# Twelve low parts of weight sums in each of three FFNs, written by ScalarE and an accumulating DMA in place of VectorE

## The chip, the cores and the metric

The kernel runs on one core of a Trainium2 chip. The metric is the device time of one execution in microseconds (us). PE is the matrix engine (TensorE), DVE is VectorE, ACT is ScalarE, POOL is GpSimd, and SP is the engine whose queue issues most of the loads.

## What is computed

The reference is a two-layer decoder trunk for 576 tokens (one sequence of 512, and eight of 8) of width 1024. Each layer is a token mixer between two half-step SwiGLU FFNs, so there are four FFNs, named (layer, place): (0,0), (0,1), (1,0), (1,1). The change is in the FFNs alone:

```python
def swiglu(h, w_gate, w_up, w_down):
    return (jax.nn.silu(h @ w_gate) * (h @ w_up)) @ w_down
...
x = x + 0.5 * swiglu(rmsnorm(x, ffn_norm[i, 0]), ffn_w_gate[i, 0], ffn_w_up[i, 0], ffn_w_down[i, 0])
```

`w_gate` and `w_up` are 1024 x 2816, `w_down` is 2816 x 1024, all float32.

## The kernel before

**Split numbers.** A float32 product is made from three matmuls of reduced operands: each operand is split into a high part (a cast to fp32r) and a low part (source minus high), and high x high, high x low and low x high are summed in PSUM. `block` (L321) does that for one 128 x 512 weight block: it takes a tile `wb` from a pool, ACT casts the high part into its first half (L326), and an engine, DVE if none is named, writes the low part `src - hi` into its second half (L327). `wb` comes from the pool `spl` with six buffers.

**Strassen products.** The gate and up projections of an FFN run over 11 column pairs, p = 0 to 10 (L541), each of 256 columns of both matrices. A pair is worked by `wino` (L373) in seven products instead of eight. `prod(i, slot)` is one product: for gate and for up, one `wb` block and 12 matmuls of 128 x 288 (L384), 24 matmuls in all. The products come in the order 0, 1, 3, 2, 4, 5, 6. Products 0, 1 and 2 read the loaded weights `raw`; products 3, 4, 5 and 6 read sums of them, `ws`, which POOL makes in `prep` (L362 to L365, four for each matrix: s0, s1, s2 and s3; product 4 reads s0, 5 reads s2, 6 reads s3). After each product DVE or ACT empties the PSUM bank (L389, L394); there are three PSUM tiles for this. `gate` (L550, L551, and the split in L418 and L419) makes the activations of the pair.

**Buffers and queues.** `load` (L330) fetches 1 MB of `w_gate` or `w_up` for a pair on SP's queue (L334) into `raw`, which has two buffers; `ws` has six. So the load for the next pair goes out when the last reader of the older one is done, and a weight sum is made when the sum whose buffer it takes has been read. After the pairs p = 2, 4, 6 and 8, `down` (L348 are its matmuls, L425 its sum into `x`) multiplies four finished columns of the activations by `w_down`; its low parts are written on POOL.

**Which FFNs.** In (0,0), (0,1) and (1,1), called plain in the code, pair 0 takes a direct path without sums (L556 to L578, the PSUM tiles emptied at L575), and the pairs 1 to 10 go through `wino`. In (1,0) all eleven do.

**What sets the order.** The program is written in the order of the loops, and the tile framework's scheduler reorders each engine's instructions within what the data and the buffers allow, by a simulated timeline (`schedule_with_timeline_sim=True`). A few instructions are pinned by `pin`. The ring for descriptors of DMAs that POOL issues is set by `dynamic_dma_scratch_size=1024`; the kernel before issues no DMA from POOL.

Of the kernel before, what the change touches and what calls it, by code (L numbers as in the profile page):

```python
# [8 lines left out]
F32 = mybir.dt.float32  # L9
F32R = mybir.dt.float32r  # L10
I32 = mybir.dt.int32
AF = mybir.ActivationFunctionType
ALU = mybir.AluOpType
# [5 lines left out]
D = 1024  # L19
# [30 lines left out]
def trunk(ctx, tc, x_prompt, x_sample, state_ssm, state_conv, state_pool,  # L50
# [5 lines left out]
    V, S, G, PE = nc.vector, nc.scalar, nc.gpsimd, nc.tensor  # L56
# [196 lines left out]
    def pin(op, on=True):  # L253
        if on:
            tc.keep_in_program_order(op)
# [64 lines left out]
    def block(src, eng=None, pool=None, late=False):  # L320
        w = (pool or spl).tile([P, 2, 4, P], F32R, name="wb")  # L321
        k = src.shape[1]
        hi, lo = w[:, 0, 0:k], w[:, 1, 0:k]
        if src.ndim == 4:
            hi, lo = [a.rearrange("p k (c f) -> p k c f", c=src.shape[2]) for a in (hi, lo)]
        S.copy(out=hi, in_=src)  # L326
        pin((eng or V).tensor_tensor(out=lo, in0=src, in1=hi.bitcast(F32), op=ALU.subtract), late)  # L327
        return w

    def load(src, shape):  # L330
# [39 lines left out]
                w[i, m] = block(src[i])  # L370
        return st, w

    def wino(wp, pre, out, hh, done, early):  # L373
        st, w = pre
        e1, e4, u2, t5 = [wp.tile([P, 2, HALF], F32, name=n) for n in ("e1", "e4", "u2", "t5")]

        def prod(i, slot):
            pt = acc_tile()
            for m in range(2):
                wb = w[i, m] if (i, m) in w else block(st[m][i])  # L380
                n = 0
                for k in range(4):
                    for j, h in ((0, 0), (0, 1), (1, 0)):
                        PE.matmul(out=pt[:, m, 0:HALF], lhsT=wb[:, j, k], rhs=hh[k, h][:, slot], start=n == 0, stop=n == 11)  # L384
                        n += 1
            return pt[:, :, 0:HALF]

        def add(o, a, b, e=V):
            e.tensor_tensor(out=o, in0=a, in1=b, op=ALU.add)  # L389

        def scale(e, o, h):
            e.tensor_tensor(out=o, in0=o, in1=psum["rb"][h].unsqueeze(1).broadcast_to(list(o.shape)), op=ALU.mult)  # L392

        S.copy(out=e1, in_=prod(0, 0))  # L394
        c11 = out[:, :, 0, 0]
        add(c11, prod(1, 1), e1)
        add(u2, prod(3, 4), e1)
        add(e4, prod(2, 6), u2)
        if early:
            early()  # L400
        scale(V, c11, 0)
        add(t5, prod(4, 3), u2)
        p7 = prod(5, 5)
        add(out[:, :, 1, 0], p7, e4)
        add(out[:, :, 1, 1], p7, t5)
        c12 = out[:, :, 0, 1]
        for h in range(2):
            scale(V, out[:, :, 1, h], h)
        done(1)
        add(c12, prod(6, 2), t5)  # L410
        scale(V, c12, 1)
        done(0)
# [84 lines left out]
    def ffn(i, s, pools, tail):  # L497
        gp, dp, fp = pools
        wg, wu, wd = kview(ffn_w_gate[i, s]), kview(ffn_w_up[i, s]), kview(ffn_w_down[i, s])

        def start(p, n):
            return prep(fp, [load(w[:, :, p * 256:(p + 1) * 256], (8, 256)) for w in (wg, wu)], n)

        plain = (i, s) != (1, 0)
# [20 lines left out]
        else:  # L525
            pre = start(0, 4)
        with ExitStack() as hs:
            hp = hs.enter_context(tc.tile_pool(name="h", bufs=1, side="right", reuse_waits="tile"))
            sqs = None
            if i + s:  # L530
                sqs = tail()
# [3 lines left out]
            hh = next(norms)  # L535
# [7 lines left out]
            for p in range(11):  # L543
                ghi = gp.tile([P, 2, T], F32R, name="ghi")
                glo = gp.tile([P, 2, T], F32R, name="glo")
                o = fp.tile([P, 2, 2, 2, HALF], F32, name="fo")
# [8 lines left out]
                if p == 0 and plain:  # L555
                    for j, h in ((0, 0), (0, 1), (1, 1), (1, 0)):  # L556
# [4 lines left out]
                        for q in range(2):  # L561
                            slot = (0, 1, 5, 2)[2 * h + q]
                            for m in range(2):
                                wb = wq[q][m]
# [4 lines left out]
                        src = pt[:, :, 0:HALF]  # L569
                        if j == 0 and i + s:  # L570
                            src = o[:, :, j, h]
# [5 lines left out]
                            gate(j)  # L577
                    next(norms)  # L578
                else:
                    wino(fp, pre if p == 0 else start(p, 0), o, hh, gate, None if p else lambda: rnorm(sqs and rnat2(sqs, D), True))  # L580
                if p % 2 == 0 and 0 < p < 10:
                    k0 = 2 * p - 4
                    down(dp, wd, k0, 4, [g[k0 + k] for k in range(4)], (0, 1, 2, 3), 0.5, False, lo_eng=G, late=p == 2)
# [652 lines left out]
```

## Time and profile before

| | us |
|---|---|
| median of the three runs | 2339.83 |
| lowest and highest run | 2336.1, 2342.46 |
| the profiled execution | 2337.29 |
| its span in the trace | 2335.6 |
| PE busy in the span | 2274.0 (97%) |
| DVE busy | 1828.9 (78%) |
| ACT busy | 1062.1 (45%) |
| POOL busy | 1030.9 (44%) |

The span is the stretch from the first to the last instruction of the profiled execution, which took 1.7 us more than its span. The engines run at the same time, so busy times don't add up to the span. A timeline row groups neighbouring instructions of one kind: its start, its length, engine, line and tile names (without buffer numbers), the count, and in square brackets how long the engine was idle before it and what ended that. A row that counts fewer matmuls than the program has can miss a record.

In the trace the second pair of FFN (0,0) begins at about 49 us, the third at about 72 us; the same stretches of (0,1) and (1,1) lie near 1040 to 1085 us and 1960 to 2005 us.

### The profile page before, as it was taken

How to read it: one execution, taken by the hardware profiler on the slowest of the kernel's cores; microseconds unless marked ns; L12 is line 12 of the kernel's file. 1: busy time of each engine (PE TensorE's matmuls, PEld its weight loads, DVE VectorE, ACT ScalarE, POOL GpSimd, SP SyncE). 2: the span in 40 equal slices, each digit the busy share in tenths (PEclk: the TensorE clock that was granted, in tenths of full speed). 3: DMA queues.
4: the chain of work that ended last, by engine and by line, in shares of the span. 5: the costliest groups of instructions: out<-in, count | busy, mean ns of one | idle time of the engine just before them, and what ended most of it. 6: DMA issues, size and time to landing. Idle time of an engine off the chain costs nothing.

```text
span 2335.6 us, 43763 instructions
## 1 busy us (share of the span) xinstructions
PE 2274.0 (97%) x17572; PEld 2233.1 (96%) x17572; DVE 1828.9 (78%) x2870; ACT 1062.1 (45%) x2004; POOL 1030.9 (44%) x796
## 2 busy tenths in 40 slices
PE   8999999999999999999999999999999999999998
PEld 7999999989999999889999999999999899999997
DVE  7887778578887777797887799777876769778866
ACT  6444335465555544443444365333443345344433
POOL 3655440334444444255555335645531325645530
PEclk9999999999999999999999999999999999999998
DMA  4323232243444443322223232332221232322221
GB/s 133 109 91 109 73 100 66 62 136 115 141 121 117 122 128 102 110 73 90 92 91 109 64 100 82 100 108 64 91 91 59 73 96 91 109 90 77 88 73 59
DMA packets 272903, 222.23 MB, mean 95 GB/s; under 512 B 8321, under 2 KB 269041, under 8 KB 272700
## 3 DMA queue, kind: packets, MB, share of 16 engines
q1 hardware_dynamic: 269172, 218.04, 30.6%
q8 instruction: 139, 2.28, 0.4%
q10 hardware_dynamic: 3528, 1.39, 0.2%
q14 instruction: 64, 0.52, 0.1%
HBM read 206.46 MB, written 12.94 MB: 94 GB/s over the span
## 4 chain that ended last, share of the span: by engine, by line
PE 74%; DVE 16%; ACT 3%; DMA 3%; issue 2%; POOL 2%; ACTq 0%; SPq 0%; DVEq 0%; POOLq 0%
PE acc L348 37%; PE acc L384 31%; DVE wb L327 4%; DVE cacc L660 1%; DVE wh L263 1%; DMA raw<-in_ffn_w_gate 1%; DVE wh L274 1%; PE acc L488 1%; POOL wb L327 1%; DVE fo L392 1%; DVE fo L389 1%; ACT m L831 1%; DVE fo L551 1%; PE misc L888 1%; DMA raw<-in_ffn_w_up 1%
## 5 line engine op out<-in xcount | busy, mean ns | idle before, releaser
L384 PE MATMUL acc<-wh,wb 128*128 128x288 f32 x6888 | 922.8, 295 | 15.1 <-DVE fo L389 5.8
L384 PEld LDWEIGHTS acc<-wh,wb 128*128 128x128 f32 x6888 | 916.0, 188 | 19.3 <-DVE wb L327 7.3
L348 PE MATMUL acc<-ghi,wb 128*128 128x288 f32 x2752 | 552.3, 295 | 6.3 <-DVE x L425 3.5
L348 PEld LDWEIGHTS acc<-ghi,wb 128*128 128x128 f32 x2752 | 441.6, 188 | 8.2 <-DVE x L425 4.4
L326 ACT CAST wb<-raw 128x512 fp32r<-128x512 f32 (+1 forms) x440 | 265.4, 607 | 352.4 <-PE acc L348 142.9
L348 PE MATMUL acc<-glo,wb 128*128 128x288 f32 x1376 | 404.2, 295 | 0.0
L348 PE MATMUL acc<-hhi,wb 128*128 128x288 f32 x1824 | 382.8, 299 | 3.3 <-DVE x L425 0.9
L327 POOL TENSOR_TENSOR wb<-raw,wb 128x512 fp32r<-128x512 f32 (+1 forms) x154 | 211.0, 1372 | 342.6 <-ACT wb L326 330.6
L327 DVE TENSOR_TENSOR wb<-ws,wb 128x512 fp32r<-128x512 f32 x328 | 328.3, 1012 | 18.1 <-ACT wb L326 17.7
L327 DVE TENSOR_TENSOR wb<-raw,wb 128x512 fp32r<-128x512 f32 (+1 forms) x286 | 274.3, 973 | 68.3 <-ACT wb L326 67.7
L326 ACT CAST wb<-ws 128x512 fp32r<-128x512 f32 x328 | 201.4, 620 | 258.4 <-PE acc L384 202.2
L348 PEld LDWEIGHTS acc<-hhi,wb 128*128 128x128 f32 x1824 | 296.8, 189 | 5.7 <-DVE x L425 1.1
L348 PE MATMUL acc<-hlo,wb 128*128 128x288 f32 x912 | 271.6, 298 | 0.0
L425 DVE SCALAR_TENSOR_TENSOR x<-acc,x 128x576 f32<-128x576 f32 x160 | 120.7, 754 | 192.0 <-PE acc L348 191.7
L365 POOL TENSOR_TENSOR ws<-raw,ws 128x512 f32<-128x512 f32 x82 | 154.8, 1888 | 243.7 <-DVE wb L327 239.4
L348 PEld LDWEIGHTS acc<-glo,wb 128*128 128x128 f32 x1376 | 257.8, 188 | 0.0
L327 POOL TENSOR_TENSOR wb<-rd,wb 128x512 fp32r<-128x512 f32 x128 | 177.4, 1398 | 161.5 <-ACT wb L326 161.5
L326 ACT CAST wb<-rd 128x512 fp32r<-128x512 f32 x196 | 113.9, 592 | 246.5 <-PE acc L348 217.5
L364 POOL TENSOR_TENSOR ws<-raw 128x512 f32<-128x512 f32 x82 | 125.2, 1526 | 166.0 <-DVE wb L327 166.0
L348 PEld LDWEIGHTS acc<-hlo,wb 128*128 128x128 f32 x912 | 172.1, 189 | 0.7 <-issue 0.2
L362 POOL TENSOR_TENSOR ws<-raw 128x512 f32<-128x512 f32 x82 | 127.2, 1552 | 70.2 <-DMA raw<-in_ffn_w_gate 66.3
L363 POOL TENSOR_TENSOR ws<-ws,raw 128x512 f32<-128x512 f32 x82 | 130.7, 1594 | 6.1
(337 smaller groups left out, 2837.9 us busy)
## 6 DMA issues: line engine op xcount, KB each, us to landing
raw<-in_ffn_w_gate SPq DMA_DIRECT2D x41, 1024.0 KB
raw<-in_ffn_w_up SPq DMA_DIRECT2D x41, 1024.0 KB
rd<-in_ffn_w_down SPq DMA_DIRECT2D x80, 512.0 KB
raw<-in_ssd_w_in SPq DMA_DIRECT2D x48, 512.0 KB
m<-ad SPq DMA_DIRECT2D x16, 576.0 KB
nat<-in_state_ssm SPq DMA_DIRECT2D x16, 512.0 KB
out<-nat SPq DMA_DIRECT2D x16, 512.0 KB
raw<-in_ssd_w_out SPq DMA_DIRECT2D x24, 256.0 KB
```

The costliest lines, as they stand in the source:

```text
L263: return V.scalar_tensor_tensor(out=o, in0=xs, scalar=g, in1=sub, op0=ALU.mult, op1=ALU.subtract)
L274: (G if slot == 3 else V).tensor_tensor(out=hh[k, 1][:, slot], in0=t[k][slot], in1=hi.bitcast(F32), op=ALU.subtract)
L326: S.copy(out=hi, in_=src)
L327: pin((eng or V).tensor_tensor(out=lo, in0=src, in1=hi.bitcast(F32), op=ALU.subtract), late)
L348: PE.matmul(out=pd[:, h, 0:HALF], lhsT=lt, rhs=a[:, h * HALF:(h + 1) * HALF], start=first and n == 0, stop=last and n == 3 * len(acts) - 1)
L362: G.tensor_tensor(out=s[0], in0=blk[2], in1=blk[3], op=ALU.add)
L363: G.tensor_tensor(out=s[1], in0=s[0], in1=blk[0], op=ALU.subtract)
L364: G.tensor_tensor(out=s[2], in0=blk[2], in1=blk[0], op=ALU.subtract)
L365: G.tensor_tensor(out=s[3], in0=blk[1], in1=s[1], op=ALU.subtract)
L384: PE.matmul(out=pt[:, m, 0:HALF], lhsT=wb[:, j, k], rhs=hh[k, h][:, slot], start=n == 0, stop=n == 11)
L389: e.tensor_tensor(out=o, in0=a, in1=b, op=ALU.add)
L425: V.scalar_tensor_tensor(out=halves(x[:, d]), in0=pt[:, :, 0:HALF], scalar=scale, in1=halves(x[:, d]), op0=ALU.mult, op1=ALU.add)
```

## The change

For products 4, 5 and 6 of the pairs p = 1 and 2 in the three plain FFNs the low part is written in another way. ACT writes the negated high part into the low half of `wb` (L328 of the changed kernel), and POOL issues a DMA that adds the source `ws` onto it (L329): 128 rows of 2 KB, 256 KB. The value is the same, `src - hi`. Two matrices by three products by two pairs by three FFNs are 36 blocks: 36 DVE instructions go, 36 ACT instructions and 36 DMAs come. From L327 on the changed kernel's lines stand four further down (L365 is L369, L384 is L388).

```diff
--- before.py
+++ after.py
@@ -324,7 +324,11 @@
         if src.ndim == 4:
             hi, lo = [a.rearrange("p k (c f) -> p k c f", c=src.shape[2]) for a in (hi, lo)]
         S.copy(out=hi, in_=src)
-        pin((eng or V).tensor_tensor(out=lo, in0=src, in1=hi.bitcast(F32), op=ALU.subtract), late)
+        if eng == "dma":
+            S.activation(out=lo, in_=hi.bitcast(F32), func=AF.Identity, scale=-1.0)
+            G.dma_start(out=lo.bitcast(F32), in_=src, accum_op=ALU.add)
+        else:
+            pin((eng or V).tensor_tensor(out=lo, in0=src, in1=hi.bitcast(F32), op=ALU.subtract), late)
         return w
 
     def load(src, shape):
@@ -370,14 +374,14 @@
                 w[i, m] = block(src[i])
         return st, w
 
-    def wino(wp, pre, out, hh, done, early):
+    def wino(wp, pre, out, hh, done, early, up=None):
         st, w = pre
         e1, e4, u2, t5 = [wp.tile([P, 2, HALF], F32, name=n) for n in ("e1", "e4", "u2", "t5")]
 
         def prod(i, slot):
             pt = acc_tile()
             for m in range(2):
-                wb = w[i, m] if (i, m) in w else block(st[m][i])
+                wb = w[i, m] if (i, m) in w else block(st[m][i], up if i > 3 else None)
                 n = 0
                 for k in range(4):
                     for j, h in ((0, 0), (0, 1), (1, 0)):
@@ -577,7 +581,7 @@
                             gate(j)
                     next(norms)
                 else:
-                    wino(fp, pre if p == 0 else start(p, 0), o, hh, gate, None if p else lambda: rnorm(sqs and rnat2(sqs, D), True))
+                    wino(fp, pre if p == 0 else start(p, 0), o, hh, gate, None if p else lambda: rnorm(sqs and rnat2(sqs, D), True), "dma" if plain and p < 3 else None)
                 if p % 2 == 0 and 0 < p < 10:
                     k0 = 2 * p - 4
                     down(dp, wd, k0, 4, [g[k0 + k] for k in range(4)], (0, 1, 2, 3), 0.5, False, lo_eng=G, late=p == 2)
```

The scheduler moves instructions near these blocks. Three places, in FFN (0,0). The number behind a tile's name tells its buffers apart; numbers of the two kernels don't match.

**POOL, second pair.** Before, the last two sums of the pair (ws_575, ws_576), then those of the third pair, from raw_825 (gate) and raw_827 (up), then the low parts of `down`:

```order
L364 TENSOR_TENSOR ws_575<-raw_563 128x512
L365 TENSOR_TENSOR ws_576<-raw_563,ws_574 128x512
L362 TENSOR_TENSOR ws_829<-raw_825 128x512
L363 TENSOR_TENSOR ws_830<-ws_829,raw_825 128x512
L364 TENSOR_TENSOR ws_831<-raw_825 128x512
L365 TENSOR_TENSOR ws_832<-raw_825,ws_830 128x512
L362 TENSOR_TENSOR ws_837<-raw_827 128x512
L363 TENSOR_TENSOR ws_838<-ws_837,raw_827 128x512
L364 TENSOR_TENSOR ws_839<-raw_827 128x512
L365 TENSOR_TENSOR ws_840<-raw_827,ws_838 128x512
L327 TENSOR_TENSOR wb_1088<-rd_1086,wb_1088 128x512
```

After, from the same place on (the third pair's raw tiles are raw_831 and raw_833). wb_715 and wb_731 are product 4 of the second pair, wb_749 and wb_765 product 5, wb_790 and wb_806 product 6:

```order
L368 TENSOR_TENSOR ws_575<-raw_563 128x512
L329 DMA wb_715<-ws_565 128x512
L329 DMA wb_731<-ws_573 128x512
L329 DMA wb_749<-ws_567 128x512
L369 TENSOR_TENSOR ws_576<-raw_563,ws_574 128x512
L366 TENSOR_TENSOR ws_835<-raw_831 128x512
L329 DMA wb_765<-ws_575 128x512
L329 DMA wb_790<-ws_568 128x512
L367 TENSOR_TENSOR ws_836<-ws_835,raw_831 128x512
L368 TENSOR_TENSOR ws_837<-raw_831 128x512
L329 DMA wb_806<-ws_576 128x512
L369 TENSOR_TENSOR ws_838<-raw_831,ws_836 128x512
```

Three issues now stand ahead of the last sum of the second pair, and the third pair's sums alternate with the other three. The next rows of POOL after, where wb_985 and wb_1001 are product 4 of the third pair, wb_1019 and wb_1035 product 5, wb_1060 and wb_1076 product 6, and raw_1341 is the gate load of the fourth pair:

```order
L366 TENSOR_TENSOR ws_843<-raw_833 128x512
L367 TENSOR_TENSOR ws_844<-ws_843,raw_833 128x512
L368 TENSOR_TENSOR ws_845<-raw_833 128x512
L329 DMA wb_985<-ws_835 128x512
L329 DMA wb_1001<-ws_843 128x512
L369 TENSOR_TENSOR ws_846<-raw_833,ws_844 128x512
L329 DMA wb_1019<-ws_837 128x512
L366 TENSOR_TENSOR ws_1345<-raw_1341 128x512
L329 DMA wb_1035<-ws_845 128x512
L329 DMA wb_1060<-ws_838 128x512
L367 TENSOR_TENSOR ws_1346<-ws_1345,raw_1341 128x512
L329 DMA wb_1076<-ws_846 128x512
```

The last three issues stand behind ws_1345, a sum of the fourth pair, which needs that pair's load.

**ACT, second pair.** Before, the casts of the product 4, 5 and 6 blocks follow each other:

```order
L326 CAST wb_730<-ws_573 128x512
L326 CAST wb_747<-ws_567 128x512
L326 CAST wb_762<-ws_575 128x512
L326 CAST wb_786<-ws_568 128x512
L326 CAST wb_801<-ws_576 128x512
L326 CAST wb_850<-raw_825 128x512
```

After, each is followed by its negation:

```order
L326 CAST wb_715<-ws_565 128x512
L328 ACTIVATE wb_715<-wb_715 128x512
L422 CAST ghi_327<-fo_329 128x576
L326 CAST wb_731<-ws_573 128x512
L328 ACTIVATE wb_731<-wb_731 128x512
L326 CAST wb_749<-ws_567 128x512
L328 ACTIVATE wb_749<-wb_749 128x512
L326 CAST wb_765<-ws_575 128x512
L328 ACTIVATE wb_765<-wb_765 128x512
L326 CAST wb_790<-ws_568 128x512
```

Nothing else on ACT moved here.

**PE, end of the second pair.** Before, product 5 (acc2_746) goes on with its second block, straight through:

```order
L384 MATMUL acc2_746<-wh31_171,wb_747 128x288
L384 MATMUL acc2_746<-wh30_170,wb_747 128x288
L384 MATMUL acc2_746<-wh00_164,wb_762 128x288
L384 MATMUL acc2_746<-wh01_165,wb_762 128x288
L384 MATMUL acc2_746<-wh00_164,wb_762 128x288
```

After, product 5 stops after two matmuls of its second block (wb_765), product 6 (acc2_789) after two of its first, and PE takes the first block of the third pair's product 0 (acc2_855, wb_856, 12 matmuls of which the first three stand here):

```order
L388 MATMUL acc2_748<-wh31_171,wb_749 128x288
L388 MATMUL acc2_748<-wh30_170,wb_749 128x288
L388 MATMUL acc2_748<-wh00_164,wb_765 128x288
L388 MATMUL acc2_748<-wh01_165,wb_765 128x288
L388 MATMUL acc2_789<-wh00_164,wb_790 128x288
L388 MATMUL acc2_789<-wh01_165,wb_790 128x288
L388 MATMUL acc2_855<-wh00_164,wb_856 128x288
L388 MATMUL acc2_855<-wh01_165,wb_856 128x288
L388 MATMUL acc2_855<-wh00_164,wb_856 128x288
```

Then two matmuls of that product's up block (wb_871, which needs the up load), and only then the rest of wb_765:

```order
L388 MATMUL acc2_855<-wh31_171,wb_856 128x288
L388 MATMUL acc2_855<-wh30_170,wb_856 128x288
L388 MATMUL acc2_855<-wh00_164,wb_871 128x288
L388 MATMUL acc2_855<-wh01_165,wb_871 128x288
L388 MATMUL acc2_748<-wh00_164,wb_765 128x288
L388 MATMUL acc2_748<-wh10_166,wb_765 128x288
```

So 14 matmuls of the third pair moved ahead of the rest of product 5.

## Rows read from the trace of the kernel before

**Rows 1.** Page: engine busy time and share, whole span.

```profile
PE 2274.0 (97%) x17572; PEld 2233.1 (96%) x17572; DVE 1828.9 (78%) x2870; ACT 1062.1 (45%) x2004; POOL 1030.9 (44%) x796
```

**Rows 2.** Busy by stretch: first FFN, second and third pair (stretch, length, engines, PEclk, DMA share, GB/s).

```profile
46.00:75.00 29.00, 26.11 (x192) 25.20 (x190) 29.00 (x42) 15.07 (x29) 14.43 (x10) 1.00 0.24 73
75.00:97.00 22.00, 20.13 (x150) 19.96 (x151) 22.00 (x28) 9.99 (x18) 14.11 (x9) 1.00 0.46 144
```

**Rows 3.** PE timeline, first FFN: start, length, line, count, idle before, releaser.

```profile
55.54 19.30 PE L384 MATMUL acc<-wh,wb 128*128 128x288 f32 x144 [1.00 <-DVE fo L575]
75.18 9.78 PE L384 MATMUL acc<-wh,wb 128*128 128x288 f32 x72 [0.33 <-DVE fo L389]
86.65 9.77 PE L384 MATMUL acc<-wh,wb 128*128 128x288 f32 x72 [1.69 <-DVE fo L389]
...
107.19 0.40 PE L348 MATMUL acc<-ghi,wb 128*128 128x288 f32 x1 [0.85 <-DVE x L425]
```

**Rows 4.** PE waits of the second FFN's stretch (1055 to 1125): total, times, longest.

```profile
PE acc L384 <- DVE fo L389: 1.7, 1, 1.7
PE acc L348 <- DVE fo L389: 1.3, 1, 1.3
PE acc L348 <- DVE x L425: 0.9, 1, 0.9
```

**Rows 5.** PE waits of the fourth FFN's stretch (1973 to 2040).

```profile
PE acc L384 <- DVE fo L389: 2.1, 2, 1.7
```

**Rows 6.** Page: the group of low parts written by DVE from weight sums.

```profile
L327 DVE TENSOR_TENSOR wb<-ws,wb 128x512 fp32r<-128x512 f32 x328 | 328.3, 1012 | 18.1 <-ACT wb L326 17.7
```

**Rows 7.** DVE timeline, first FFN, second pair: low parts among it.

```profile
58.94 0.68 DVE L327 TENSOR_TENSOR wb<-ws,wb 128x512 fp32r<-128x512 f32 x1
...
61.48 1.11 DVE L327 TENSOR_TENSOR wb<-ws,wb 128x512 fp32r<-128x512 f32 x1
...
63.85 3.04 DVE L327 TENSOR_TENSOR wb<-ws,wb 128x512 fp32r<-128x512 f32 x2
```

**Rows 8.** ACT timeline, first FFN, second pair.

```profile
57.06 0.62 ACT L326 CAST wb<-ws 128x512 fp32r<-128x512 f32 x1
58.45 0.68 ACT L418 CAST ghi<-fo 128x576 fp32r<-128x576 f32 x1 [0.77 <-DVE fo L551]
59.03 2.23 ACT L326 CAST wb<-ws 128x512 fp32r<-128x512 f32 x4
...
67.83 1.66 ACT L326 CAST wb<-raw 128x512 fp32r<-128x512 f32 x3 [3.42 <-DMA raw<-in_ffn_w_up]
```

**Rows 9.** POOL timeline, first FFN, second pair.

```profile
59.77 2.28 POOL L365 TENSOR_TENSOR ws<-raw,ws 128x512 f32<-128x512 f32 x1 [3.91 <-DVE wb L327]
63.34 1.30 POOL L362 TENSOR_TENSOR ws<-raw 128x512 f32<-128x512 f32 x1 [1.29 <-DVE fo L392]
...
66.30 1.74 POOL L364 TENSOR_TENSOR ws<-raw 128x512 f32<-128x512 f32 x1
```

**Rows 10.** SP's queue, first FFN: issues of weight loads.

```profile
57.82 0.37 SPq L334 DMA_DIRECT2D raw<-in_ffn_w_gate  x1
62.07 0.37 SPq L334 DMA_DIRECT2D raw<-in_ffn_w_up  x1
81.48 0.37 SPq L334 DMA_DIRECT2D raw<-in_ffn_w_gate  x1
```

**Rows 11.** Busy by stretch while the first load runs (columns as in rows 2).

```profile
59.50:62.50 3.00, 3.00 (x25) 3.00 (x25) 3.00 (x5) 2.04 (x5) 2.28 (x1) 1.00 0.99 326
```

**Rows 12.** Page: DMA queues: packets, MB, share of 16 engines.

```profile
q1 hardware_dynamic: 269172, 218.04, 30.6%
q8 instruction: 139, 2.28, 0.4%
q10 hardware_dynamic: 3528, 1.39, 0.2%
q14 instruction: 64, 0.52, 0.1%
```

## The prediction

> **What bounds the kernel now.** Over the whole span PE is busy 97% of the time and DVE 78% [rows 1], so PE sets the end and DVE looks as if it had room. The stretches that the change touches read otherwise. In the second and third column pair of the first FFN, DVE is busy in every one of 29 and 22 us, while PE loses some there [rows 2]; the clock is granted in full, so none of that loss is clock. What PE waits for stands in its timeline: from 75 us on it stops 0.33, 1.69 and 0.85 us, each time for a DVE instruction that empties a PSUM tile [rows 3]. DVE has been given more than it can do in these pairs, so it comes late to the tile that PE needs next. The other two FFNs show the same: 1.7 + 1.3 + 0.9 = 3.9 us [rows 4], and 2.1 us with the same 1.3 and 0.9 again, 4.3 us [rows 5]. With 0.33 + 1.69 + 0.85 = 2.9 us of the first that makes **11.1 us**, 0.47% of the time. It is all that taking work off DVE can bring here.
>
> **What is removed.** 36 DVE instructions of about 1.0 us [rows 6], in the first FFN's second pair between 0.68 and 1.5 us each [rows 7]. Six for a pair take some 6 us out of 22, more than the longest wait of 1.69 us, so I take all 11.1 us as gone. The last waits, 0.85 and 0.9 us before L348, come after DVE's full stretch and may stay: then the gain is 11.1 - 2.7 = 8.4 us.
>
> **What ACT gets.** 36 instructions on 128 x 512, which I price as its casts: four in 2.23 us, 0.56 us each [rows 8]. ACT is busy 10 of the 22 us of the third pair [rows 2], and the six take 3.4 us more: they lie beside other work. But each stands in the chain from cast to low part, and the casts behind them on ACT come 0.56 us later each.
>
> **What the DMA costs.** The trace has no DMA issued by POOL: of its four queues two carry instructions, and the two others the loads and stores of SP and ACT [rows 12]. So I bound the time L from POOL's turn to the landed low part. A 1 MB load, issued at 57.82, is followed by POOL's first sum of it at 63.34 [rows 9, 10], 5.5 us; the DMA engines move 326 GB/s at 99% share [rows 11], 3.2 us for 1 MB, which leaves 2.3 us fixed, the 0.37 us of issue included. The second load, issued at 62.07 and read by ACT at 67.83 [rows 8, 10], gives 5.76 - 3.2 = 2.5 us. At that rate 256 KB pass in 0.8 us. Low end: one pass, as a load, 2.3 + 0.8 = 3.1 us. High end: three passes (read source, read target, write target) and an issue as long as a POOL instruction, 1.30 us [rows 9] in place of 0.37: 2.5 + 0.9 + 2.4 = 5.8 us. A gain on the load's row isn't to be had, since each transfer still has an issue, a way and a landing. I take two passes, since two reads feed one write: **L = 3.9 us**, and 1.0 us of POOL for each issue, between 0.37 and 1.30. Through DVE the same step took 0.68 us when DVE had its turn [rows 7].
>
> The Trainium skill, "DMA: Bandwidth & Descriptors", section "Anatomy of one DMA — SWDGE (gpsimd) path", fits 2.0 us plus the bytes at 436 GB/s for such a DMA, 2.6 us for 256 KB as an estimate; no run here shows it yet. By it the sum would end with rival A below.
>
> **Who waits, second pair.** PE does 144 matmuls in 19.30 us [rows 3], 0.134 us each, 1.61 us a block, 3.22 us a product. Two products after 55.54 it starts product 4, at 61.97; a block's low part is wanted two matmuls in. Wanted, with no new wait: wb_715 at 62.2, wb_731 at 63.85, wb_749 at 65.5. Then come the 18 matmuls that the order now puts there, and wb_765 at 69.2, wb_790 at 70.5, wb_806 at 72.2. Ready:
> ACT casts wb_715 at 57.06 [rows 8], negates it by 58.2, and it lands at 62.1: in time. wb_731 is cast after ghi at 59.03 [rows 8], negated by 60.15, landed by 64.05, while the gate load has the DMA engines at 99% [rows 11]. That adds between nothing and 1.6 us; with 0.8, PE waits **1.0 us**. wb_749, negated by 61.3, lands in time.
> POOL's last sum of the pair, L365, ran at 59.77 [rows 9]. Now it stands behind three issues and takes the buffer that the first DMA reads, so it starts at 62.1 and ends near 63.7. It is the last reader of the up buffer, so the up load goes out 1.7 us later than at 62.07 [rows 10], and ACT's cast of it at 69.5 instead of 67.83 [rows 8], done at 70.1. PE wants the up block of the hoisted product at 68.9 + 1.0: **0.2 us**.
> On POOL wb_765's issue follows one more sum, and wb_806's two more: sums of 1.30 us, 1.74 beside DVE [rows 9], 1.6 taken. wb_765 starts at 65.3 and lands at 69.2, wb_790 a turn later, both in time; wb_806 starts at 70.5 and lands at 74.4, wanted at 72.2 + 1.2: **1.0 us**. Second pair: 2.2 us.
>
> **Who waits, third pair.** Product 4 would start at 75.18 + 9.78 = 84.96 [rows 3], less the 0.33 us wait, plus 2.2: 86.8. POOL's sum ws_844 waits for wb_806's landing, so wb_985 goes out at 77.6 and lands at 81.5, wb_1001 a turn later, both early. ws_846 waits for wb_985 and ends at 83.1; wb_1019 lands at 87.0, wanted at 90.3. Next on POOL stands ws_1345, a sum of the fourth pair, and behind it the last three issues. The gate load it needs went out at 81.48 [rows 10]; 1.9 us later now, and 5.5 us to its reader: 88.9, done at 90.2. wb_1035 lands at 94.1, wanted at 91.9: **2.2 us**. wb_1060 follows in time; wb_1076, behind one more sum, lands at 97.7, wanted at 97.3: **0.4 us**. Third pair: 2.6 us.
>
> **The sum.** New waits 3 x (2.2 + 2.6) = 14.4 us, old ones 11.1 us: +3.3 us. On the profiled execution, 2337.29 (1.7 us of it outside its span of 2335.6), that is 2340.6. The median of the runs, 2339.83, lies 2.5 us above the profiled execution, so I predict **2343**. The same steps with L = 3.1 give waits of 0.4 (the up load) and 1.4 (wb_1035) in an FFN, 5.4 us in three: 2334. With L = 5.8 they give 1.9 + 1.5 + 0.4 + 2.2 in the second pair and 0.7 + 3.8 in the third, 31.5 us: 2360. So a microsecond of L is worth about 9.7 us, more than anything on DVE. A measurement of this kernel can tell 0.3%, 7 us, from no change.
>
> **Rival A, the transfers land in time.** If L is below about 3 us, or the fourth pair's load comes 2 us earlier because DVE frees its buffer sooner, the new waits nearly vanish and most of the 11.1 us stays as gain: 2337.3 - 11.1 + 2.5 = 2329 at the best, 2333 at the edge of what can be told. For it speaks that the DMA engines are free for more than half of both stretches (shares 0.24 and 0.46) [rows 2]; against it that the shortest way of a load leaves 2.3 us before the first byte of data is counted.
>
> **Rival B, the adding transfer is slow.** Slower: each low part goes through the DMA engines with reads on both sides, and PE uses up a block in 1.61 us. If one such transfer holds the engines for longer than 2.2 us (L above 4.5), low parts come late in nearly every block, each late landing also holds a POOL sum, and with it a load. By the slope it is slower by over 7 us from L = 4.5, 2360 at L = 5.8, and 2370 at 6.8. For it: no row shows an adding transfer, and six of them and two loads share a pair's 22 us; against it: at two passes the twelve of two pairs take 19 us of 51.
>
> **Rival C, POOL's issue is held up beside DVE.** POOL's sums take 1.30 us alone and 1.74 beside DVE [rows 9], and DVE will still be busy most of these stretches. If an issue is stretched by the same 0.45 us, and mostly one waits behind another, low parts land 0.9 us later: 14.4 + 0.9 x 9.7 - 11.1 = +12 us, 2352.
> The Trainium skill, "SBUF — State Buffer", section "Who interferes with whom", tells of a DMA issued from GpSimd that took 3100 instead of 620 ns beside DVE; 2.5 us more on each L would be some 24 us, 2367 as an estimate. It also infers that tensor_tensor, which is most of what DVE runs here, doesn't do it, so I give it little.
>
> **Rival D, it doesn't do what it says.** PE's waits stay although DVE is relieved, since the emptying instructions wait for something else on DVE: no gain, 14.4 us of cost, 2354. Against it stands DVE without a gap in both stretches.
>
> **How the numbers follow.** L between 3.0 and 4.5, within 0.3%: 0.44. Rival A, faster: 0.17. Rival B 0.30, C 0.06 and D 0.03, slower: 0.39. Range: below 2330 lies the best third of A, 0.06; above 2364 the slow third of B and the tail of C, 0.12. So 2330 to 2364 holds 0.82.
>
> **What would show it.** Right: a POOL queue of 36 transfers and 9.4 MB on the page; DVE no longer full in both pairs; the L389 waits gone from PE; in their place waits for low parts (DMA onto wb) at wb_731 and wb_806, and the longest at wb_1035, about 2 us, behind ws_1345; the up load of the third pair some 1.7 us late. L is read from issue to landing: near 3.9 us I am right in size; above 4.5, B; issues far over 1.0 us on POOL, C; L389 waits still there, D. Wrong altogether would be a wait of PE outside these pairs, such as SP or POOL carrying a delay into the fourth pair.

## The result and the profile after

The changed kernel takes 2376.86 us (median of six), against 2337.89 of the kernel before: 39 us more, a ratio of 1.0169 with an interval of 1.0159 to 1.0179. The prediction was 2343 with a range of 2330 to 2364: the sign of the sum came out, its size didn't. The profiled execution took 2382.25 us, its span is 2380.5, so 44.9 us longer than the span before; the medians differ by 39.

The page of the changed kernel: engines, the queue that is new, one group (busy, mean ns | idle before, releaser), and the new transfers (KB each, median us from issue to landing).

```profile
PE 2285.9 (96%) x17572; PEld 2245.2 (94%) x17572; DVE 1824.6 (77%) x2834; ACT 1084.1 (46%) x2040; POOL 1040.5 (44%) x832
...
q0 software_dynamic: 5184, 9.44, 2.2%
...
L331 DVE TENSOR_TENSOR wb<-raw,wb 128x512 fp32r<-128x512 f32 (+1 forms) x286 | 303.2, 1074 | 98.5 <-ACT wb L326 97.8
...
wb<-ws POOLq DMA_DIRECT2D x36, 256.0 KB, 5.2
```

The 36 transfers are there, 9.44 MB. Their share of 2.2% of 16 engines is 0.022 x 2380.5 / 36 = 1.45 us of engine time for each. They land 5.2 us after their issue in the middle, 3.5 at the earliest and 7.7 at the latest. The row to look at is the last but one: DVE's low parts from `raw`, which the change doesn't touch, take 303.2 us. The same 286 instructions took 274.3 us before, and none of them was long (count, then ns least/median/most, first and last start, in the kernel before):

```profile
L327 DVE TENSOR_TENSOR wb<-raw,wb x286: 407/692/1787, 20.1 to 2260.2; 128x512 fp32r<-128x512 f32 x139, 128x256 fp32r<-128x256 f32 x4
```

PE's waits of the whole changed kernel (total, times, longest):

```profile
PE acc L352 <- DVE t L393: 21.6, 2, 11.0
PE acc L388 <- DMA wb<-ws: 10.7, 5, 5.6
...
PE acc L388 <- DVE t L393: 5.8, 2, 3.0
...
PE acc L388 <- DVE fo L393: 0.7, 1, 0.7
```

The old waits for `fo` are nearly gone: of the 2.0, 1.7 and 2.1 us before L388 in the three FFNs [rows 3 to 5], 0.7 us is left. The landings cost 10.7 us. But 21.6 and 5.8 us went to something that stood nowhere in the prediction: PE waits for t5, the sum that DVE makes in L393 from a PSUM tile, up to 11.0 us at a time. The two losses lie in different places. The 27.4 us for t5 fall on the second and the fourth FFN, 13.6 and 14.0 us (the parts are rounded). In the first FFN PE doesn't wait for t5; it waits 7.9 of the 10.7 us for landings, most of it at once, for the transfer that POOL issued at 92.67 and that landed 7.6 us later:

```profile
100.31 3.22 PE L388 MATMUL acc<-wh,wb 128*128 128x288 f32 x12 [5.62 <-DMA wb<-ws]
```

Why DVE was so late is seen in the third pair of the second FFN. DVE's timeline there:

```profile
1089.37 12.42 DVE L331 TENSOR_TENSOR wb<-raw,wb 128x512 fp32r<-128x512 f32 x1 [2.09 <-ACT wb L326]
1101.71 0.74 DVE L393 TENSOR_TENSOR t<-acc,u 128x576 f32<-128x576 f32 x1
```

POOL's timeline over the same time:

```profile
1087.47 1.30 POOL L366 TENSOR_TENSOR ws<-raw 128x512 f32<-128x512 f32 x1
1088.70 1.79 POOL L329 DMA_DIRECT2D wb<-ws  x2
1089.86 1.95 POOL L367 TENSOR_TENSOR ws<-ws,raw 128x512 f32<-128x512 f32 x1
1091.10 1.92 POOL L368 TENSOR_TENSOR ws<-raw 128x512 f32<-128x512 f32 x1
1092.32 1.54 POOL L329 DMA_DIRECT2D wb<-ws  x1
1092.93 5.87 POOL L331 TENSOR_TENSOR wb<-rd,wb 128x512 fp32r<-128x512 f32 x4
1097.82 2.20 POOL L369 TENSOR_TENSOR ws<-raw,ws 128x512 f32<-128x512 f32 x1
1099.04 2.19 POOL L366 TENSOR_TENSOR ws<-raw 128x512 f32<-128x512 f32 x1
```

And PE's:

```profile
1102.51 0.61 PE L352 MATMUL acc<-ghi,wb 128*128 128x288 f32 x1 [10.69 <-DVE t L393]
1103.15 4.77 PE L388 MATMUL acc<-wh,wb 128*128 128x288 f32 x22
```

One DVE low part on 128 x 512, 0.68 us where it has its turn [rows 7], stands at 12.42 us. It begins at 1089.37, while POOL issues two transfers, and it ends at 1101.79, half a microsecond after POOL's last instruction of that run (1099.04 + 2.19 = 1101.23). In between POOL has eight instructions and three issues without a gap: each instruction starts 1.2 us after the one before and each is 1.9 to 2.2 us long, so by these rows the next has been taken before the last is done (the profile's spans on POOL are rough). The three transfers are not what DVE waits for: the last of them had landed by 1096.5, 4.6 us before DVE got its turn. t5 stands behind the low part on DVE, PE behind t5: 10.69 us. When PE starts again its clock is down:

```profile
1101.70:1108.00 6.30, 5.49 (x26) 5.49 (x27) 4.16 (x8) 0.88 (x2) 0.00 (x0) 0.59 0.01 2
```

(Stretch, length, busy time of PE, PEld, DVE, ACT and POOL, granted clock, DMA share, GB/s.) Around PE's restart the granted clock is 0.59 of the full 2.4 GHz, a mix of it and the 1.2 GHz level, and the 22 matmuls from 1103.15 on take 4.77 us, where 22 x 0.134 [rows 3] = 2.95 us would do at the full clock: 1.8 us more. Over the whole kernel PE's busy time for the same 17572 matmuls is 2285.9 us against 2274.0 [rows 1]. These 11.9 us are, as an estimate, what the lower clock cost, and the other 33.0 of the 44.9 us are time in which PE stood.

Where the time went by FFN, from SP's issues of weight loads in the changed kernel:

```profile
59.17 0.37 SPq L338 DMA_DIRECT2D raw<-in_ffn_w_gate  x1
67.22 0.37 SPq L338 DMA_DIRECT2D raw<-in_ffn_w_up  x1
...
139.88 0.37 SPq L338 DMA_DIRECT2D raw<-in_ffn_w_gate  x1
...
1052.45 0.37 SPq L338 DMA_DIRECT2D raw<-in_ffn_w_gate  x1
...
1137.41 0.37 SPq L338 DMA_DIRECT2D raw<-in_ffn_w_gate  x1
```

From the third pair's gate load at 59.17 to the fifth pair's at 139.88 are 80.7 us, in the second FFN 85.0; the same stretches took 68.5 (57.82 [rows 10] to 126.35) and 71.5 us before. With the third FFN's 84.4 against 69.6 that is 12.2 + 13.5 + 14.9 = 40.6 of the 44.9 us. The rest, 1.4 us before the first of them and 2.7 between the first two FFNs, lies outside the changed pairs, and its cause was not looked for.

### The profile page after: what moved, and what is told of

It reads as the page before. It is cut to its first block, busy times and chain, and to the rows that moved or that the text cites. A ratio compares the mean times of both kernels' runs of the same rounds, so it can differ in the third digit from the quotient of the medians.

```text
span 2380.5 us, 43855 instructions
## 1 busy us (share of the span) xinstructions
PE 2285.9 (96%) x17572; PEld 2245.2 (94%) x17572; DVE 1824.6 (77%) x2834; ACT 1084.1 (46%) x2040; POOL 1040.5 (44%) x832
## 3 DMA queue, kind: packets, MB, share of 16 engines
q0 software_dynamic: 5184, 9.44, 2.2%
## 4 chain that ended last, share of the span: by engine, by line
PE 73%; DVE 13%; issue 5%; DMA 4%; ACT 3%; POOL 1%; SPq 0%; ACTq 0%; DVEq 0%; POOLq 0%
PE acc L352 36%; PE acc L388 32%; DVE wb L331 2%; DVE cacc L664 2%; DMA wb<-ws 1%; DVE wh L263 1%; PE acc L492 1%; ACT m L835 1%; DMA raw<-in_ffn_w_gate 1%; ACT wb L326 1%; DVE wh L274 1%; DVE ws L1122 1%; PE misc L892 1%; DMA raw<-in_ffn_w_up 1%; POOL wb L331 1%
## 5 line engine op out<-in xcount | busy, mean ns | idle before, releaser
L388 PE MATMUL acc<-wh,wb 128*128 128x288 f32 x6888 | 933.3, 297 | 26.7 <-DMA wb<-ws 10.7
L388 PEld LDWEIGHTS acc<-wh,wb 128*128 128x128 f32 x6888 | 925.3, 190 | 31.5 <-DMA wb<-ws 11.8
L352 PE MATMUL acc<-ghi,wb 128*128 128x288 f32 x2752 | 553.6, 296 | 24.5 <-DVE t L393 21.6
L352 PEld LDWEIGHTS acc<-ghi,wb 128*128 128x128 f32 x2752 | 443.0, 188 | 25.9 <-DVE t L393 22.1
L352 PE MATMUL acc<-glo,wb 128*128 128x288 f32 x1376 | 405.2, 295 | 0.0
L352 PE MATMUL acc<-hhi,wb 128*128 128x288 f32 x1824 | 383.3, 300 | 2.5 <-DVE m L1097 0.8
L331 DVE TENSOR_TENSOR wb<-raw,wb 128x512 fp32r<-128x512 f32 (+1 forms) x286 | 303.2, 1074 | 98.5 <-ACT wb L326 97.8
L352 PEld LDWEIGHTS acc<-hhi,wb 128*128 128x128 f32 x1824 | 297.5, 189 | 4.7 <-DVE m L1097 1.1
L331 DVE TENSOR_TENSOR wb<-ws,wb 128x512 fp32r<-128x512 f32 x292 | 285.2, 987 | 17.4 <-ACT wb L326 16.7
L352 PE MATMUL acc<-hlo,wb 128*128 128x288 f32 x912 | 272.1, 298 | 0.0
L429 DVE SCALAR_TENSOR_TENSOR x<-acc,x 128x576 f32<-128x576 f32 x160 | 120.5, 754 | 195.5 <-PE acc L352 195.4
L352 PEld LDWEIGHTS acc<-glo,wb 128*128 128x128 f32 x1376 | 258.8, 188 | 0.0
L369 POOL TENSOR_TENSOR ws<-raw,ws 128x512 f32<-128x512 f32 x82 | 148.0, 1805 | 227.9 <-DVE wb L331 210.8
L352 PEld LDWEIGHTS acc<-hlo,wb 128*128 128x128 f32 x912 | 172.6, 189 | 0.7 <-issue 0.2
```

Source lines behind the costliest of these rows:

```text
L352: PE.matmul(out=pd[:, h, 0:HALF], lhsT=lt, rhs=a[:, h * HALF:(h + 1) * HALF], start=first and n == 0, stop=last and n == 3 * len(acts) - 1)
L369: G.tensor_tensor(out=s[3], in0=blk[1], in1=s[1], op=ALU.subtract)
L429: V.scalar_tensor_tensor(out=halves(x[:, d]), in0=pt[:, :, 0:HALF], scalar=scale, in1=halves(x[:, d]), op0=ALU.mult, op1=ALU.add)
```

## The experiments

Two theories for the loss were put against each other. **Lockout**: after POOL has issued a DMA, it runs its next instructions without a gap, and a DVE instruction with two operands in SBUF waits until that run ends. **Slow transfers** (rival B of the prediction): low parts land late, and sums, loads and PE wait for them. All runs are the changed kernel with an edit or two, compared with the kernel before on the same chip.

**A plain copy in place of the adding DMA, same order (copy_pool).**

```diff
-            G.dma_start(out=lo.bitcast(F32), in_=src, accum_op=ALU.add)
+            G.dma_start(out=lo.bitcast(F32), in_=src)
```

> The POOL DMA onto the low half copies the source instead of adding it (so the low part is wrong by the high part). Every engine's order is that of the changed kernel, word for word. Lockout theory: after a DMA issue POOL runs its next instructions without a gap, and a DVE instruction with two SBUF operands waits until that run ends; adding has no part in it: the longest DVE low part stays above 10 us, PE's waits for L393's t5 stay near 27 us, 2370 to 2380 us. Rival, the adding transfer itself holds DVE's operands up: the longest DVE low part falls below 2 us, 2340 to 2350 us. Rival, slow transfers are what costs: issue to landing falls from 5.2 us by a pass, 0.5 to 0.8 us, and the time by 5 to 8 us.

2348.39 us, ratio 1.0044 (1.003 to 1.0059): 29 us of the 39 went away with the adding, though no instruction moved. The page's rows of the transfers, and DVE's low parts from `raw` over the whole kernel (count, then ns least/median/most, first and last start):

```profile
q0 software_dynamic: 2880, 9.44, 1.1%
...
wb<-ws POOLq DMA_DIRECT2D x36, 256.0 KB, 4.4
```

```profile
L331 DVE TENSOR_TENSOR wb<-raw,wb x286: 408/693/6649, 19.1 to 2271.2; 128x512 fp32r<-128x512 f32 x139, 128x256 fp32r<-128x256 f32 x4
```

2880 packets instead of 5184, half the engine share (0.72 us for each), landings at 4.4 instead of 5.2 us; the longest low part 6.65 instead of 12.42 us. None of the three expectations holds as it was written: the time is the one expected if adding alone held DVE up, yet four lockouts are still there, 3.5 to 6.65 us long. PE's rows tell where the 29 us (33.9 between the profiled executions) went: it waits 7.1 us for t5 instead of 27.4 and 7.2 for landings instead of 10.7, and its busy time is 2276.5 instead of 2285.9. So shorter waits for t5 are the largest part. The same place in the second FFN shows what differs. POOL:

```profile
1075.16 1.10 POOL L329 DMA_DIRECT2D wb<-ws  x2
1076.28 1.29 POOL L367 TENSOR_TENSOR ws<-ws,raw 128x512 f32<-128x512 f32 x1
1077.52 1.28 POOL L368 TENSOR_TENSOR ws<-raw 128x512 f32<-128x512 f32 x1
1078.74 0.56 POOL L329 DMA_DIRECT2D wb<-ws  x1
1079.32 6.17 POOL L331 TENSOR_TENSOR wb<-rd,wb 128x512 fp32r<-128x512 f32 x4
```

DVE:

```profile
1075.82 3.91 DVE L331 TENSOR_TENSOR wb<-raw,wb 128x512 fp32r<-128x512 f32 x1 [2.13 <-ACT wb L326]
1079.65 0.74 DVE L393 TENSOR_TENSOR t<-acc,u 128x576 f32<-128x576 f32 x1
```

An issue of a plain copy takes 0.55 us and the next instruction starts when it ends; an adding one takes 0.88 us and the next starts 0.6 us after its start. With the copy DVE's low part waits through two sums and gets its turn at the following issue, at about 1079; from there on the two share, POOL's four low parts taking 6.17 us, 1.54 each. With adding, the issue at 1092.32 left no such opening, and DVE waited for the whole run.

**The copies from SP's queue (copy_sp).**

```diff
-            G.dma_start(out=lo.bitcast(F32), in_=src, accum_op=ALU.add)
+            nc.sync.dma_start(out=lo.bitcast(F32), in_=src)
```

> The same 36 transfers as plain copies from SP's queue instead of POOL's (low part wrong by the high part). POOL's order is that of the kernel before. Lockout theory: no DVE low part longer than 2 us, no wait for L393's t5 of 3 us or more, and only the waits for landings stay, 10 us or less: 2335 to 2350 us. Slow-transfer theory: landings as late as with POOL, about 5 us from issue, 2360 us or more.

2350.36 us, ratio 1.0042 (1.0027 to 1.0058). DVE's low parts from `raw`, and PE's wait for landings:

```profile
L331 DVE TENSOR_TENSOR wb<-raw,wb x286: 406/692/1802, 19.2 to 2278.8; 128x512 fp32r<-128x512 f32 x139, 128x256 fp32r<-128x256 f32 x4
```

```profile
PE acc L388 <- DMA wb<-ws: 15.9, 8, 2.6
```

No low part over 1.8 us, no wait for t5 among PE's waits: without POOL's issues no lockout. PE loses 15.9 us to landings, more than the 10 expected. This is what late low parts cost by themselves: if the old 11.1 us are gone, 15.9 - 11.1 = 4.8 us, and PE's busy time is 5.4 us longer (2279.4 against 2274.0), together within the 6 to 14 that the interval says.

**POOL writes the low parts itself (lo_pool).**

```diff
-                    wino(... "dma" if plain and p < 3 else None)
+                    wino(... G if plain and p < 3 else None)
```

> The 36 low parts are written by POOL's tensor_tensor, with no DMA and no negation on ACT; POOL has as many instructions in a row as in the changed kernel, in nearly the same order. If a DMA issue is needed for the lockout: no DVE low part over 2.5 us, 2335 to 2350 us. If a backlog on POOL is enough: DVE low parts of 5 us and more, 2355 us and more.

2338.99 us, ratio 0.9999 (0.999 to 1.0009): the same as before. POOL has more instructions in a row than in the changed kernel, in nearly that order: in the second FFN 22 from 1063.79 to 1097.25 without a gap above 0.07 us, against 13 entries from 1086.22 to 1101.23. Still no DVE low part is over 1.83 us. POOL's timeline in the first FFN's second pair:

```profile
63.48 1.29 POOL L366 TENSOR_TENSOR ws<-raw 128x512 f32<-128x512 f32 x1
64.74 2.99 POOL L331 TENSOR_TENSOR wb<-ws,wb 128x512 fp32r<-128x512 f32 x2
67.69 1.74 POOL L367 TENSOR_TENSOR ws<-ws,raw 128x512 f32<-128x512 f32 x1
```

DVE's:

```profile
64.79 1.79 DVE L331 TENSOR_TENSOR wb<-raw,wb 128x512 fp32r<-128x512 f32 x1 [0.47 <-POOL ws L366]
```

DVE's low part comes at 64.79, just after POOL started one of its own, with POOL's next one ready. It waits for that one instruction, 1.2 us, and then goes: 1.79 us in all. So a backlog on POOL and a DVE that comes second don't make a lockout; the DMA issue does. PE's waits, whole kernel:

```profile
PE acc L388 <- POOL wb L331: 5.4, 4, 1.6
...
PE acc L388 <- DVE fo L393: 2.4, 3, 1.1
```

The old waits shrank to 2.4 us, and 5.4 us for POOL came.

**ACT's negation alone (neg_act_add_dve).**

```diff
-            G.dma_start(out=lo.bitcast(F32), in_=src, accum_op=ALU.add)
+            V.tensor_tensor(out=lo, in0=src, in1=lo.bitcast(F32), op=ALU.add)
```

> ACT negates as in the changed kernel, but DVE adds the source, so no DMA: this is ACT's part alone. If the 36 ACT instructions lie beside other work, as the prediction has it: within 5 us of the kernel before, 2335 to 2343 us, with DVE's old waits of L389 still there. If the longer chain from cast to low part costs by itself: 2350 us or more.

2344.14 us, ratio 1.0026 (1.0016 to 1.0036), so 4 to 8 us above the kernel before. That is between the two expectations: the 36 instructions and the longer chain through them cost something, and the run doesn't tell one from the other. In the profiled execution PE's waits for `fo` before L388 are 7.8 us, 2.4 at the longest, against 5.8 and 1.7 before; that the low parts, later on DVE, push the emptying of PSUM back is likely, but not shown.

**The transfers beside the work (side_acc).**

```diff
+    spare = [dram.tile([P, 4, P], F32, name=f"spare{n}") for n in range(6)]
...
-            S.activation(out=lo, in_=hi.bitcast(F32), func=AF.Identity, scale=-1.0)
-            G.dma_start(out=lo.bitcast(F32), in_=src, accum_op=ALU.add)
+            V.tensor_tensor(out=lo, in0=src, in1=hi.bitcast(F32), op=ALU.subtract)
+            side.append(0)
+            G.dma_start(out=spare[len(side) % 6], in_=src, accum_op=ALU.add)
```

> The 36 low parts stay on DVE, as before; beside each, POOL issues an accumulating DMA of the same weight sum onto a spare buffer in HBM that nobody reads (six buffers, filled at the start by six extra loads of 256 KB, which may cost some us there). No engine waits for what these transfers bring, so late low parts are out of it. Lockout theory: DVE instructions with two SBUF operands are held up again, several of 3 us and more in pairs 1 and 2 of the three FFNs, and PE loses 3 us or more an FFN to DVE. Slow-transfer theory: the longest DVE low part stays under 2 us and the pairs take as long as before.

A single run, 2372.07 us, of which some 7 us lie before the changed pairs (the second pair's gate load goes out at 36.64 instead of 29.82). No engine waits for what these transfers bring. DVE and POOL in the third pair of the second FFN:

```profile
1089.47 9.01 DVE L332 TENSOR_TENSOR wb<-ws,wb 128x512 fp32r<-128x512 f32 x2
```

```profile
1089.11 0.89 POOL L334 DMA_DIRECT2D spare<-ws  x1 [0.41 <-POOL ws L374]
1089.72 5.30 POOL L336 TENSOR_TENSOR wb<-rd,wb 128x512 fp32r<-128x512 f32 x4
1094.69 1.55 POOL L371 TENSOR_TENSOR ws<-raw 128x512 f32<-128x512 f32 x1
1096.32 1.63 POOL L372 TENSOR_TENSOR ws<-ws,raw 128x512 f32<-128x512 f32 x1
```

Two DVE low parts take 9.01 us, the first of them 7.32, to 1096.79. Less the 0.68 us that it takes with its turn, that turn came at about 1096.1, where POOL's run behind one issue, five instructions long, has its first gap (1094.69 + 1.55 = 1096.24, the next at 1096.32). Ten DVE instructions of 3 us and more lie in the three FFNs, where the kernel before has none, and each begins 0.2 to 0.6 us after the start of an issue. PE waits 18.4 us for DVE's low parts before L393, against 5.6 before. From the third pair's gate load on, the three FFNs take 74.8, 78.0 and 75.9 us, 6.3 to 6.5 us more than before. Slow transfers can't do that: nothing hangs on them, apart from the buffers that they read.

**A shorter run (down_dve).**

```diff
-                    down(... lo_eng=G, late=p == 2)
+                    down(... lo_eng=None if plain and p == 2 else G, late=p == 2)
```

> The changed kernel with the sixteen low parts of the third pair's down projection on DVE in the three plain FFNs instead of POOL. It takes four instructions of 1.22 us out of POOL's run behind the last issues. Lockout theory: the longest DVE low part falls from 12.4 to about 7.5 us, and the time by about 3 x 5 us, to 2357 to 2366 us. Slow-transfer theory: landings are as late as they were, 2370 us or more.

2397.37 us, ratio 1.0248 (1.023 to 1.0265): 20 us slower than the changed kernel. The lockout theory had it faster; the time lies in the range of the slow-transfer theory, 2370 us or more, and PE's waits for landings are what they were, 10.6 us, but that theory has no reason for the 20 us. What it was made for came: the same low part in the second FFN's third pair, now with two sums and an issue behind the two issues,

```profile
1096.41 4.21 DVE L331 TENSOR_TENSOR wb<-raw,wb 128x512 fp32r<-128x512 f32 x1 [2.23 <-ACT wb L326]
```

is 4.21 us long instead of 12.42 (7.5 were expected), and PE's wait for t5 there fell from 10.7 to 2.6 us. But DVE's part of the down projection, pinned in program order by `late`, now goes in step with PE. PE's wait for these low parts over the whole kernel:

```profile
PE acc L352 <- DVE wb L331: 15.9, 3, 5.6
```

Before, there was no such wait at L348. So the lockout got shorter, as its theory says, and the loss came back from another place; since the time didn't fall, this run doesn't show what the shorter lockout was worth.

**Second or third pair alone (p1_only, p2_only).** The condition `p < 3` became `p == 1` and `p == 2`.

> The change in the second pair alone. From the changed kernel's waits there (2.9 us for t5 and 0.4 us for a landing in the second changed FFN, against 0.4 us of old waits that end), 2 to 4 us an FFN: 2340 to 2350 us by both theories; lockout theory: the longest DVE low part about 4 us.

> The change in the third pair alone. Lockout theory: the long run of POOL behind the last issues of the third pair is all there, so is a DVE low part of 10 us or more, and three quarters of the loss: 2362 to 2372 us. Slow-transfer theory: half of the transfers, half of the loss or less, 2350 to 2358 us.

2347.04 us, ratio 1.0032 (1.0019 to 1.0045), and 2368.05, ratio 1.0122 (1.0107 to 1.0137). Against 39 us for both, the third pair alone costs 28 and the second alone 7. DVE's low parts from `raw` in p2_only:

```profile
L331 DVE TENSOR_TENSOR wb<-raw,wb x286: 409/692/9639, 19.0 to 2288.4; 128x512 fp32r<-128x512 f32 x139, 128x256 fp32r<-128x256 f32 x4
```

9.64 us at the most, where the down projection's low parts follow POOL's issues; in p1_only it is 4.24 us, where POOL has only sums of the next pair behind them. So the lockouts are as expected, and the time of p2_only lies in the lockout theory's range. But the time comes from elsewhere. PE's largest wait there:

```profile
PE acc L388 <- DMA wb<-ws: 16.6, 6, 3.8
```

PE doesn't wait for t5 at all, and 4.2 us for `fo` of L393. Its busy time is 14.4 us longer than before (2288.4 against 2274.0), again for the same matmuls. The three lockouts (9.50, 9.64 and 9.57 us) begin after t5 of that pair is made (in the second FFN t5 at 1083.45, the lockout at 1088.56), and PE has other work meanwhile. The agreement with the lockout theory's 2362 to 2372 us is luck: in this order it is late landings, 7.6 to 7.8 us from issue at the latest, that PE waits for.

**Twelve transfers instead of 36 (prod6_only).** The condition `i > 3` became `i > 5`.

> The change for product 6 alone: 12 accumulating DMAs instead of 36. Lockout theory: POOL's run behind the two issues of the third pair is four or more instructions, so DVE is held up 4 us or more there, 2343 to 2355 us. Slow-transfer theory: a third of the transfers, those wanted last, hidden: 2334 to 2342 us.

2346.5 us, ratio 1.0033 (1.0021 to 1.0045).

```profile
L331 DVE TENSOR_TENSOR wb<-raw,wb x286: 408/692/7502, 19.7 to 2266.5; 128x512 fp32r<-128x512 f32 x139, 128x256 fp32r<-128x256 f32 x4
```

Two issues in the third pair are enough for a low part of 7.4 to 7.5 us in each of the three FFNs. PE waits 9.0 us for landings and 6.1 us for `fo` before L352, 2.6 before. Fewer transfers of this kind are still slower than none, and both kinds of wait are there.

**A version that gains? (lo_pool45, lo_pool4.)** In lo_pool it was product 6 that PE waited for, so its low parts went back to DVE: `i in (4, 5)`, and `i == 4`.

> Low parts of products 4 and 5 of the two pairs on POOL's tensor_tensor, those of product 6 on DVE as before; no DMA, no negation. With all three products on POOL, PE's waits for POOL were those of product 6 (1.2 to 1.6 us a pair). If the old waits for DVE end (11 us) and no such wait comes: 2329 to 2336 us. If DVE's and POOL's instructions slow each other by as much as is moved: 2337 to 2341 us.

> The same for product 4 alone, two low parts a pair. Two DVE instructions of about 1 us less a pair against an old wait of 1.7 us: 2332 to 2337 us if DVE's lateness is the whole of that wait, 2337 to 2341 us if not.

2340.32 us, ratio 1.0008 (0.9999 to 1.0017), and 2344.68, ratio 1.0029 (1.0018 to 1.0041): the same, and 0.3% slower. In lo_pool45 the waits for POOL's low parts are gone, but PE waits 5.9 us for `x` (L429) and 2.9 us for `fo` before L388. What DVE is spared comes back as other waits; that POOL's longer work beside DVE makes them is likely, but not shown, and neither is why product 4 alone is slower than 4 and 5. None of the kernels that were run beats the one before.

## Why the prediction was wrong

**What bounds, and the gain: right.** DVE was late, and relieving it ended most of the old waits: over the whole kernel before L388 from 5.8 to 0.7 us, and before L352 for `x` (L429) from 4.3 to 0.8 us. The 2.6 us for `fo` before L352, in the second and fourth FFN, are gone as well; 1.9 us of that kind are new, in the first FFN, behind a lockout. One reading was off: the row of 3.04 us in [rows 7] holds low parts of 1.34 and 1.77 us, not two of 1.5. Nothing hangs on it.

**ACT: a little too cheap.** "They lie beside other work" put the 36 instructions at nothing; neg_act_add_dve shows 4 to 8 us for them together with the longer chain to DVE's add.

**The transfer: mis-sized in one part.** Two passes were right: 1.45 us of engine time against 1.6 taken, and half of it, 0.72, for a copy. The issue of 1.0 us was 0.88. The earliest landing, 3.5 us, leaves 2.1 us beside them, near the 2.3 of the prediction; the middle one leaves 3.7, the latest 6.2. So what was too small is the typical L, 5.2 us and not 3.9, beyond the 4.5 at which rival B starts, and what stretched it is not shown; loads and other transfers were under way at the same time. The Trainium skill, "DMA: Bandwidth & Descriptors", section "Anatomy of one DMA — SWDGE (gpsimd) path", gives 2.6 us for this size as an estimate by its fit. The runs show 4.4 us for the plain copy and 5.2 for the adding one, so the measurement decides.

**The waits for landings: near in size by luck.** PE's waits for landings are 10.7 us, the sum had 14.4. But with L = 5.2 the prediction's own slope gives 5.4 + 2.1 x 9.7 = 26 us of them; that no more came fits PE's being held up elsewhere, which was not tested. They were not where they were looked for either: the longest, 5.6 us, is in the first FFN at wb_1019, the third transfer of the pair, which was to be in time, and not at wb_1035. A correct L would have moved the forecast to 26 - 11.1 = +15 us, 2354, and rival B would have been called. It would still have been 22 us short. Rival B was no idle thought: in p2_only landings are the largest wait, 16.6 us. The up load of the third pair went out 3.8 us late (67.22 against 62.07 [rows 10], less the 1.35 us by which that FFN began later), not 1.7.

**The step that failed** is the count of who waits. POOL's sums were priced for those who wait for their results, and rival C asked whether DVE holds up POOL's issues ("POOL's issue is held up beside DVE"), never the reverse. The change puts issues in front of POOL's sums and low parts, lets them pile up behind landings, and then lets them run without a gap, and DVE, which was to be relieved, stands still for as long: 3.5 and 9.6 us in the first FFN, 4.2 and 12.4 in each of the other two. In those two t5 stood behind the held low part, which gave PE 21.6 + 5.8 = 27.4 us of waits; in the first it didn't, and the 9.6 us cost PE 1.9. A second term was put at nothing: the sum prices a wait of PE at its length, but the clock fell while PE stood, and PE was busy 11.9 us longer for the same matmuls. Shown: without issues on POOL no DVE low part is over 1.9 us (before, copy_sp, lo_pool, neg_act_add_dve); with issues that nobody waits for the lockouts are there (side_acc); and where POOL's run behind the issue is shorter, so is the lockout (12.4 and 4.2 us, changed kernel and down_dve; 9.6 and 4.2, p2_only and p1_only). What a lockout costs depends on what PE needs from DVE meanwhile: 10.7 us for one of 12.4, and 0.9 us of waits for `fo` behind one of 9.6 (p2_only, second FFN). The rows that could have warned: 1.30 us alone against 1.74 beside DVE [rows 9] says that the two engines take turns at something, and a rival on who gets the turn should have gone both ways.

The Trainium skill, "SBUF — State Buffer", section "Who interferes with whom", says that a DVE instruction with two inputs in SBUF contends with a POOL instruction that reads SBUF, and the page has it that whichever starts first keeps the other out for the whole instruction. The trace agrees as to which instructions: those of L393, with one operand in PSUM, took 0.76 us at most in the whole changed kernel, one of them in a run of POOL behind two issues (70.58, below; POOL's sum runs there from 70.42, for 1.97 us). For the length it does not: after an issue the other was kept out for a whole run of up to 11 entries of POOL's timeline, not for one instruction.

**What stays open.** Why an issue changes the taking of turns was not shown. The overlap of POOL's rows after an adding issue (the next starts 0.6 to 1.0 us before the last ends) goes with the longer lockouts, but in copy_pool a lockout of 6.65 us stands in a run whose rows overlap by 0.05 us only. The overlap is then no full explanation, and the link is argued, not shown. Nor does an adding issue always shut DVE out: in the first FFN of the changed kernel a low part with two SBUF operands came at 94.58, just after the first of two issues (94.52), and was done in 0.82 us. The two rows of DVE:

```profile
70.58 0.76 DVE L393 TENSOR_TENSOR t<-acc,u 128x576 f32<-128x576 f32 x1 [0.60 <-PE acc L388]
...
94.58 0.82 DVE L331 TENSOR_TENSOR wb<-raw,wb 128x512 fp32r<-128x512 f32 x1 [2.39 <-ACT wb L326]
```

How much of the 39 us the lockouts make by themselves was not separated either: no run has the adding transfers from POOL without lockouts.

## What to carry to other kernels

Before work goes from a full engine to a DMA issued by POOL, look at what POOL runs behind the issue and which instructions of DVE read two operands from SBUF at that time: they may stand still until POOL's run ends, and PE with them. Price the landing from a transfer on that very queue, or leave 4.4 us for a copy of 256 KB and 5.2 for an adding one, up to 7.7 here. Ask as well what PE will need from DVE while DVE stands: that, and not the length of the standstill, is the cost. Relieving the engine that bounds a stretch is worth its waits at most (here 0.47%), so any new chain that costs more than that has lost before it begins.

## What the runs showed of the hardware that was not expected

- After a DMA issue on POOL, a DVE instruction on 128 x 512 with two SBUF operands took up to 12.42 us, against 0.68 alone and 1.82 at the most in the kernel before. It ended with POOL's run, whose last entry can be an issue, at a gap of 0.08 us in it, or at the issue of a plain copy. Without issues on POOL, 22 of its instructions in a row held no low part of DVE longer than 1.83 us.
- Adding in a DMA doubled its engine time (1.45 against 0.72 us for 256 KB), took 5184 instead of 2880 packets for 36 transfers, and made the issue on POOL 0.88 instead of 0.55 us long.
- From 1101.70 to 1108.00, around PE's restart after 10.7 us of standing still, the granted clock was 0.59, and 22 matmuls took 4.77 us instead of 2.95.
